# Down projection of an MLP as 2x2 blocks with seven products, its sums shared between VectorE and GpSimd

## The chip, the cores and the metric

The kernel runs on one core of a Trainium2 chip. The metric is the device time of one execution in microseconds; a kernel's time is the median of its runs. Engine names in the profile: PE is TensorE's matmuls, PEld its weight loads, DVE is VectorE, ACT is ScalarE, POOL is GpSimd, SP is SyncE, which issues most of the DMAs.

## The reference

One layer of a hybrid block on 512 tokens of width 2048: a gated-DeltaNet group and an RWKV-7 group, an output projection, cross attention to 256 memory tokens, and an MLP. What matters here is the end of it:

```python
D_MODEL = 2048; SEQ = 512; D_FF = 4 * D_MODEL
def reference(...):
    ...
    hn = _rmsnorm(h, norm_mlp[l])
    h = h + jnp.square(jax.nn.relu(hn @ mlp_w_up[l])) @ mlp_w_down[l]
    return _rmsnorm(h, norm_final)
```

All inputs and the output are float32. The kernel keeps that precision by splitting each operand of a product into a high part and a residue (lo = x - hi) and adding three matmuls: hi x hi, hi x lo, lo x hi.

## The kernel before

Everything is held transposed: features on the 128 partitions, the 512 tokens along the free dimension. The residual stream is 16 tiles `hres[n]` of 128x512.

**Splitting.** `split` writes the high part on ScalarE (L125, a cast) and the residue on VectorE (L126, a subtraction of two SBUF tiles). Weights come as raw tiles of 128x1024 (`wraw`, three buffers) and are split into `whi` and `wlo`, two buffers each, so the split of one block of weights can only start when TensorE has done with the block before the last. `mm` (L117) is the matmul, so all matmuls of the later stages have that line.

**Up** (strassen, 32 blocks `up0` to `up31`) multiplies 2x2 blocks with seven products instead of eight (Winograd's form). The blocks are halves of the tokens (`HA`, `HB`, 256 columns each) against pairs of feature rows. The sums of weights and of products are on VectorE (L1335). In the blocks 4 to 30 the products are "wide": high and low part of the activation lie side by side in one tile and one matmul takes 512 columns for hi x (hi, lo). In the others all matmuls have 256 columns, three for each weight block. Each result is squared and written to memory (`Ud`).

**Down** has eight parts of 1024 hidden rows, `e` = 0 to 7. The parts 0 to 6 are plain products: for each of the 16 output tiles `n`, the weights `w_dn[e, n]` are loaded and split, 24 matmuls of 512 columns go into one bank of PSUM (`dn{e}_{n}`), and VectorE adds the bank to `hres[n]` (L1722). Between these, `usplit` reads back the next part's hidden activations, multiplies them by `rstd` on VectorE (L1681) and splits them (`uh`, `ul`, 32 buffers of 128x512 under the name `act`, 24 more under `actb`). Part 7 goes token half by token half, so that the final norm and the output can begin early.

**Order of work.** Up and the parts 0 to 6 of down are put in order by a scheduler that takes the instructions as the code issues them and moves an engine's instruction ahead when its operands are there. Each engine then works its own queue strictly in order. Part 7 has its VectorE and ScalarE order as written. Tiles of one name share a fixed number of buffers, and a new tile waits until the readers of the old one are done.

GpSimd works in the first third only: prefix scans and masks of the two mixers.

Of the kernel before, what the change touches and what calls it, by code (L numbers as in the profile page):

```python
# [9 lines left out]
F32 = mybir.dt.float32  # L10
F32R = mybir.dt.float32r
AF = mybir.ActivationFunctionType
ALU = mybir.AluOpType
# [4 lines left out]
P = 128  # L18
T = 512
M = 256  # L20
KD = 16
# [52 lines left out]
def build(tc, I, out):  # L74
    nc = tc.nc
    V, S, GP, PE = nc.vector, nc.scalar, nc.gpsimd, nc.tensor
# [36 lines left out]
    def psb(nm, tag="mx", bufs=2):  # L113
        return tile_of(ps, [P, 512], F32, tag, nm, bufs)
# [29 lines left out]
    def wload(src):  # L144
        raw = wraw()
        nc.sync.dma_start(raw if len(src.shape) == 2 else raw.rearrange("p (a b) -> p a b", b=P), src)
        hi, lo = wsplit()
        split(raw, hi, lo)
        return hi, lo

    def gemm(pt, wsrc, nk, hi, lo):
        for h in range(nk // 8):
            wh, wl = wload(wsrc[:, h * 1024:(h + 1) * 1024] if nk > 8 else wsrc)
            for kk in range(8):
                k = h * 8 + kk
                sl = slice(kk * P, (kk + 1) * P)
                mm(pt, wh[:, sl], hi[k], start=(k == 0), stop=False)
                mm(pt, wh[:, sl], lo[k], start=False, stop=False)
                mm(pt, wl[:, sl], hi[k], start=False, stop=(k == nk - 1))
# [174 lines left out]
    def act_tile(nm, dt=F32R):  # L334
        return tile_of(pa, [P, 512], dt, "act", nm, 32)
# [5 lines left out]
    rstd = pc.tile([P, T], F32, name="rstd")  # L341
# [4 lines left out]
    cnt = [0]  # L346
# [87 lines left out]
    acc = tl("r")  # L434
# [807 lines left out]
    pm_cm.__exit__(None, None, None)  # L1242
    pq_cm.__exit__(None, None, None)
    ph = es.enter_context(tc.tile_pool(name="ph", bufs=1, reuse_waits="tile"))
    hres = [ph.tile([P, T], F32, tag=f"h{k}", name=f"h{k}", bufs=1) for k in range(16)]

    def btile(nm, dt=F32R):
        return ph.tile([P, 512], dt, tag="actb", name=nm, bufs=24)
# [11 lines left out]
    HA, HB = slice(0, M), slice(M, 2 * M)  # L1260
    comb = [[None] * 8 for _ in range(7)]

    B11, T1, T2, T3, T4, B22, B21 = range(7)
# [152 lines left out]
    banks, wts = {}, {}  # L1416
# [63 lines left out]
    for s in range(64):  # L1480
# [8 lines left out]
        if s > 1 and vsteps[s - 2][0] == "v" and vsteps[s - 2][2]:  # L1489
            n = vsteps[s - 2][1]  # L1490
# [92 lines left out]
    for g in range(2):  # L1583
        banks = (("mm", 2), ("mg", 2), ("mg", 2), ("mm", 2)), (("scr", 1), ("scg", 1), ("mm", 2), ("mm", 2))
        pts = [psb(f"sc{g}_{t}", *banks[g][t]) for t in range(4)]
        for n2 in range(8):
            cnt[0] += 1
            raw = pw.tile([P, 1024], F32, tag="wraw", name=f"kqr{cnt[0]}", bufs=NWR)
# [83 lines left out]
    def usplit(f):  # L1672
        if f >= 8:
            r = sl2()
        elif f % 2:
            r = ph.tile([P, T], F32, tag="acc", name=f"ur{f}", bufs=1)
        else:
            r = pu.tile([P, T], F32, tag="ur", name=f"ur{f}", bufs=1)
        nc.sync.dma_start(r, Ud[f // 2][:, f % 2, :])
        if f >= 8:  # L1680
            V.tensor_tensor(out=r, in0=r, in1=rstd, op=ALU.mult)  # L1681
        hi, lo = act_tile(f"uh{f}"), act_tile(f"ul{f}")
        if f < 56:
            split(r, hi, lo)
        else:
            for t, half in ((hi, HA), (lo, HB)):
                split(r[:, half], t[:, HA], t[:, HB])
        uhl[0].append(hi)
        uhl[1].append(lo)
# [3 lines left out]
    for p in range(32):  # L1693
# [9 lines left out]
        def used(i):  # L1703
# [5 lines left out]
            if p == 31 and i in (T1, T2, T3):  # L1709
                for f in (range(0, 3), range(3, 6), range(6, 8))[i - T1]:  # L1710
# [1 line left out]

        strassen(f"up{p}", (pu, 1024), [I["w_up"][p, i] for i in range(4)], list(range(8)), square, used, p == 0,
                 range(7) if 3 < p < 31 else ())
    for e in range(7):
        uh, ul = uhl[0][e * 8:], uhl[1][e * 8:]
        for n in range(KD):
            if n % 2 == 0:
                usplit(e * 8 + 8 + n // 2)
            pt = psb(f"dn{e}_{n}", "mm", 2)  # L1720
            gemm(pt, I["w_dn"][e, n], 8, uh, ul)
            V.tensor_tensor(out=hres[n], in0=hres[n], in1=pt, op=ALU.add)  # L1722

# [7 lines left out]
    def multiply(s):  # L1733

        n, half = where_[s]
        outs[s] = pt = psb(f"dn7_{s}", "mm", 2)
        wh, wl = wts[s]
        u = uhl[half is HB][56:]
        for k in range(8):
            sl = slice(k * P, k * P + P)  # L1740
            if s < 31:
                mm(pt, wh[:, sl], u[k], start=k == 0, stop=False)
            else:
                mm(pt[:, HA], wh[:, sl], u[k][:, HA], start=k == 0, stop=False)
                mm(pt[:, HA], wh[:, sl], u[k][:, HB], start=False, stop=False)
            mm(pt[:, HA], wl[:, sl], u[k][:, HA], start=False, stop=k == 7)
# [26 lines left out]
                               op0=ALU.mult, op1=ALU.mult)  # L1773
        (nc.sync if n % 2 or half is HA else nc.scalar).dma_start(out[n][:, half], h)

    wts[0] = wload(I["w_dn"][7, 0])
    for s in range(32):
        if s:
            collect(s - 1)
        if s < 31:  # L1780
            wts[s + 1] = wload(I["w_dn"][7, where_[s + 1][0]])
        if s:
            squared(s - 1)
            summed(s - 1)
        multiply(s)
        if s == 17:
            S.activation(rstd[:, HA], total(HA, sqs[15]), AF.Ln, bias=b_eps6, scale=1.0 / 2048)
        elif s == 18:
            S.activation(rstd[:, HA], rstd[:, HA], AF.Exp, scale=-0.5)
            ready += range(KD)  # L1790
        elif s == 22:
            S.activation(rcol[:, 0:1], rstd[:, 0:1], AF.Ln)
        for _ in range((s > 18) + (18 < s < 24)):
            if ready:
                scaled(ready.pop(0), HA)
# [10 lines left out]
def layout(inputs):  # L1806
    a = {k: np.asarray(v) for k, v in inputs.items()}
    f = np.float32
    D = 2048
    GW = 1024  # L1810
    d = {}
    d["xT"] = np.ascontiguousarray(a["x"][0].T.reshape(16, P, T).transpose(1, 0, 2))
    d["memT"] = np.ascontiguousarray(a["mem"][0].T.reshape(16, P, M).transpose(1, 0, 2))

    def tiles(w):
        kd, nd = w.shape[0] // P, w.shape[1] // P
        return np.ascontiguousarray(
            w.reshape(kd, P, nd, P).transpose(2, 1, 0, 3).reshape(nd, P, kd * P))

    w = a["w_in"][0]  # L1820
    r0 = 4 * GW + 16
    zero = lambda n: np.zeros((D, n), f)
    o0 = r0 + 3 * GW
    blocks = [w[:, o0:o0 + 128], w[:, o0 + 128:o0 + 256],
              w[:, o0 + 256:o0 + 288], w[:, 4 * GW:4 * GW + 8], zero(24),
              w[:, 4 * GW + 8:4 * GW + 16], zero(56)]
    for j in range(8):
        s = slice(j * P, (j + 1) * P)
        blocks += [w[:, r0:][:, s], w[:, r0 + GW:][:, s], w[:, r0 + 2 * GW:][:, s]]
        blocks += [w[:, i * GW:][:, s] for i in (1, 0, 2, 3)]  # L1830
    d["w_in"] = tiles(np.concatenate(blocks, 1))

    prm = np.zeros((P, NPRM), f)

    def put(name, arr, rows=slice(0, P)):
        o, n = PRM[name]
        prm[rows, o:o + n] = arr

    cols = lambda v: v.reshape(-1, P).T
    for n in ("norm_mix", "norm_xattn", "norm_mem", "norm_mlp"):  # L1840
        put(n, cols(a[n][0]))
    put("norm_final", cols(a["norm_final"]))
    mu = a["rwkv_mu"][0]
    mt = np.zeros((27, P), f)
    mt[0] = mu[3072:3200]
    mt[1] = mu[3200:3328]
    mt[2, :32] = mu[3328:3360]
    for j in range(8):
        for i in range(3):
            mt[3 + 3 * j + i] = mu[i * GW + j * P:i * GW + (j + 1) * P]  # L1850
    put("mu", mt.T)
    for n, k in (("w0", "rwkv_w0"), ("a0", "rwkv_a0"), ("kk", "rwkv_k_k"), ("ka", "rwkv_k_a"),
                 ("lnw", "rwkv_ln_w"), ("lnb", "rwkv_ln_b")):
        put(n, cols(a[k][0]))
    put("rk", cols(a["rwkv_r_k"][0].reshape(-1)))
    cw = a["gdn_conv_w"][0]
    put("conv", cw.reshape(4, 24, P).transpose(2, 1, 0).reshape(P, 96))
    put("gnw", a["gdn_norm_w"][0].reshape(P, 1))
    put("dtb", a["gdn_dt_bias"][0].reshape(8, 1), slice(32, 40))
    put("alog", a["gdn_A_log"][0].reshape(8, 1), slice(32, 40))  # L1860
    d["prm"] = prm
    d["cst"] = constants()
    d["w2a2"] = np.concatenate([a["rwkv_w2"][0], a["rwkv_a2"][0]], 0)
    g2 = a["rwkv_g2"][0]
    d["g2a"] = np.ascontiguousarray(g2[:128])
    d["g2b"] = np.ascontiguousarray(g2[128:])
    d["wk"] = tiles(a["xattn_wk"][0])
    d["wv"] = tiles(a["xattn_wv"][0])
    d["wqT"] = tiles(np.ascontiguousarray(a["xattn_wq"][0].T))
    wo = a["xattn_wo"][0]  # L1870
    d["wo"] = np.ascontiguousarray(
        wo.reshape(4, 4, P, 4, 512).transpose(3, 0, 2, 1, 4).reshape(4, 4, P, 2048))

    def blocks7(w):

        v = w.reshape(w.shape[0] // 256, 2, P, w.shape[1] // 256, 2, P)
        t = [v[:, k, :, :, m].transpose(2, 1, 0, 3) for m, k in ((0, 0), (1, 0), (1, 1), (0, 1))]
        return np.ascontiguousarray(np.stack(t, 1).reshape(w.shape[1] // 256, 4, P, -1))

    d["w_out"] = blocks7(a["w_out"][0])  # L1880
    d["w_up"] = blocks7(a["mlp_w_up"][0])
    wd = a["mlp_w_down"][0]
    d["w_dn"] = np.ascontiguousarray(
        wd.reshape(8, 8, P, 16, P).transpose(0, 3, 2, 1, 4).reshape(8, 16, P, 1024))
    return d


# [14 lines left out]
```

## Time and profile before

| | us |
|---|---|
| runs (3): median, lowest, highest | 2997.26, 2996.05, 2998.96 |
| profiled execution | 2995.97 |
| its span, first to last instruction | 2994.2 |
| mean granted TensorE clock | 0.999 |

| engine | busy us | share of the span |
|---|---|---|
| PE | 2963.1 | 99% |
| PEld | 2501.3 | 84% |
| DVE | 2125.9 | 71% |
| ACT | 1452.6 | 49% |
| POOL | 209.6 | 7% |

All times in lines of the profile count from the span's start. A line of a group reads: source line, engine, operation, out<-in by the program's names, shapes, count, then busy us and mean ns of one, then the idle time of the engine before these and who ended it. A line of the order in time reads: start, duration, engine, line, operation, out<-in. Matmuls are pipelined, so their pace is read from their starts. An instruction of VectorE is recorded with its tail, which overlaps the start of the next.

### The profile page before, as it was taken

How to read it: one execution, taken by the hardware profiler on the slowest of the kernel's cores; microseconds unless marked ns; L12 is line 12 of the kernel's file. 1: busy time of each engine (PE TensorE's matmuls, PEld its weight loads, DVE VectorE, ACT ScalarE, POOL GpSimd, SP SyncE). 2: the span in 40 equal slices, each digit the busy share in tenths (PEclk: the TensorE clock that was granted, in tenths of full speed). 3: DMA queues.
4: the chain of work that ended last, by engine and by line, in shares of the span. 5: the costliest groups of instructions: out<-in, count | busy, mean ns of one | idle time of the engine just before them, and what ended most of it. 6: DMA issues, size and time to landing. Idle time of an engine off the chain costs nothing.

```text
span 2994.2 us, 49167 instructions
## 1 busy us (share of the span) xinstructions
PE 2963.1 (99%) x19420; PEld 2501.3 (84%) x19420; DVE 2125.9 (71%) x3390; ACT 1452.6 (49%) x2133; POOL 209.6 (7%) x547
## 2 busy tenths in 40 slices
PE   9999999999999999999999999999999999999998
PEld 7887877877878888789978988888888888888887
DVE  7676676676778667679748999999997444444458
ACT  6455555555556565654446555555554222222234
POOL 0212311311312000000000000000000000000000
PEclk9999999999999999999999999999999999999999
DMA  5333333433435597763323444344444333333345
GB/s 183 105 89 81 104 88 83 103 87 82 130 89 164 176 280 244 257 227 126 104 79 99 148 135 141 128 134 140 132 137 159 127 127 103 115 126 127 116 127 183
DMA packets 226999, 402.91 MB, mean 135 GB/s; under 512 B 91912, under 2 KB 115724, under 8 KB 226768
## 3 DMA queue, kind: packets, MB, share of 16 engines
q1 hardware_dynamic: 211792, 373.54, 40.7%
q10 hardware_dynamic: 14976, 26.22, 2.3%
q8 instruction: 153, 2.51, 0.4%
q14 instruction: 78, 0.64, 0.1%
HBM read 352.10 MB, written 47.59 MB: 133 GB/s over the span
## 4 chain that ended last, share of the span: by engine, by line
PE 90%; DMA 2%; DVE 2%; ACT 1%; issue 1%; POOL 0%; ACTq 0%; SPq 0%; DVEq 0%; POOLq 0%
PE dn L117 23%; PE up L117 21%; PE py L244 18%; PE op L117 5%; PE kq L244 3%; PE vp L117 3%; PE at L117 3%; PE sc L117 3%; PE kp L244 3%; DMA wraw<-in_wo 1%; PE vo L117 1%; PE rs L244 1%; PE gs L244 1%; ACT whi L125 1%; PE pgB L244 0%
## 5 line engine op out<-in xcount | busy, mean ns | idle before, releaser
L125 ACT CAST whi<-wraw 128x1024 fp32r<-128x1024 f32 x384 | 404.0, 1052 | 758.6 <-PE dn L117 440.0
L126 DVE TENSOR_TENSOR wlo<-wraw,whi 128x1024 fp32r<-128x1024 f32 x384 | 469.3, 1222 | 75.3 <-ACT whi L125 72.5
L117 PE MATMUL up<-cb,whi 128*128 128x512 f32 (+1 forms) x2072 | 453.1, 363 | 0.8 <-ACT whi L125 0.8
L117 PE MATMUL dn<-ul,whi 128*128 128x512 f32 (+1 forms) x1032 | 394.0, 388 | 0.0
L117 PE MATMUL dn<-uh,whi 128*128 128x512 f32 x1024 | 393.8, 390 | 0.0
L117 PE MATMUL dn<-uh,wlo 128*128 128x512 f32 (+1 forms) x1024 | 384.5, 375 | 0.0
L117 PEld LDWEIGHTS up<-cb,whi 128*128 128x128 f32 x2072 | 342.2, 190 | 50.4 <-ACT whi L125 1.0
L244 PE MATMUL py<-xhi,whi 128*128 128x512 f32 x928 | 372.9, 402 | 6.8 <-ACT xhi L244 6.8
L244 PE MATMUL py<-xlo,whi 128*128 128x512 f32 x928 | 374.0, 403 | 0.3 <-DVE xlo L244 0.3
L244 PE MATMUL py<-xhi,wlo 128*128 128x512 f32 x928 | 373.1, 402 | 0.0
L1722 DVE TENSOR_TENSOR h<-h,dn 128x512 f32<-128x512 f32 x112 | 76.9, 686 | 298.4 <-PE dn L117 298.4
L244 DVE TENSOR_TENSOR wlo<-wraw,whi 128x1024 fp32r<-128x1024 f32 (+1 forms) x180 | 222.3, 1235 | 84.1 <-ACT whi L244 79.3
L244 ACT CAST whi<-wraw 128x1024 fp32r<-128x1024 f32 (+1 forms) x180 | 188.1, 1045 | 192.1 <-PE py L244 137.8
L117 PEld LDWEIGHTS up<-cb,wlo 128*128 128x128 f32 x1792 | 242.8, 191 | 16.1 <-DVE wlo L126 1.4
L117 PE MATMUL up<-cb,wlo 128*128 128x256 f32 x1792 | 251.2, 282 | 1.2 <-DVE wlo L126 1.2
L117 PEld LDWEIGHTS dn<-ul,whi 128*128 128x128 f32 x1032 | 193.2, 188 | 39.9
L117 PEld LDWEIGHTS dn<-uh,whi 128*128 128x128 f32 x1024 | 192.2, 188 | 40.9
L117 PEld LDWEIGHTS dn<-uh,wlo 128*128 128x128 f32 x1024 | 192.3, 188 | 35.1 <-DVE wlo L126 0.2
L244 PEld LDWEIGHTS py<-xhi,whi 128*128 128x128 f32 x928 | 175.1, 189 | 42.7 <-ACT xhi L244 7.2
L1335 DVE TENSOR_TENSOR sl<-sl,up 128x256 f32<-128x256 f32 x440 | 175.3, 417 | 45.7 <-PE up L117 43.2
L244 PEld LDWEIGHTS py<-xlo,whi 128*128 128x128 f32 x928 | 175.0, 189 | 35.7 <-DVE xlo L244 1.5
L244 PEld LDWEIGHTS py<-xhi,wlo 128*128 128x128 f32 x928 | 175.1, 189 | 34.4 <-issue 2.1
(848 smaller groups left out, 5195.8 us busy)
## 6 DMA issues: line engine op xcount, KB each, us to landing
wraw<-in_w_dn SPq DMA_DIRECT2D x144, 512.0 KB, 3.5
wraw<-in_w_up SPq DMA_DIRECT2D x128, 512.0 KB, 3.6
wraw<-in_w_in SPq DMA_DIRECT2D x116, 512.0 KB, 3.7
wraw<-in_wk SPq DMA_DIRECT2D x32, 512.0 KB, 3.6
wraw<-in_wqT SPq DMA_DIRECT2D x32, 512.0 KB, 5.2
wraw<-in_wv SPq DMA_DIRECT2D x32, 512.0 KB, 4.7
wraw<-in_wo SPq DMA_DIRECT2D x32, 512.0 KB, 5.7
wraw<-in_w_out SPq DMA_DIRECT2D x32, 512.0 KB, 3.6
```

Of the source, the lines that this page charges most:

```text
L117: PE.matmul(o, l, r, start=start, stop=stop)
L125: S.copy(hi, src)
L126: V.tensor_tensor(out=lo, in0=src, in1=hi.bitcast(F32), op=ALU.subtract)
L244: f(*a, **k)
L1335: V.tensor_tensor(out=o, in0=a, in1=b, op=op)
L1722: V.tensor_tensor(out=hres[n], in0=hres[n], in1=pt, op=ALU.add)
```

## The change

The parts 1 to 6 of down become 2x2 blocks with seven products.

- A *unit* is one part and one group `g` of four output tiles. Its four weight blocks (`w_dm`, 128x1024 each) are loaded raw; VectorE makes three sums of them (L1793, L1795, L1804), GpSimd one difference (L1799). Each of the seven products splits its weights and issues 24 matmuls of 256 columns into one bank of PSUM, two output tiles side by side.
- The results: `p1` and `p5` are copied out of PSUM by ScalarE, `u2` and `u3` are made by VectorE (L1782) from PSUM and a copy; GpSimd adds these copies to the residual, six additions of 512 columns a unit (L1778); VectorE adds `p2`, `p3` and `p4` from PSUM itself.
- The activations of the next part are made beside the unit (`downpair`): read back, multiplied by `rstd` on GpSimd (L1733), four differences on GpSimd (L1737), seven splits of 256 columns on ScalarE and VectorE.
- The residual tiles lie in pairs, `hp[i]` of 128x2x512, so that one addition reaches two output tiles in one token half.
- Part 0 stays plain, with the first `downpair` groups beside it; part 7 is the same with other indices. The multiplications by `rstd` that `usplit` did on VectorE go to GpSimd.

```diff
-    hres = [ph.tile([P, T], F32, tag=f"h{k}", name=f"h{k}", bufs=1) for k in range(16)]
+    hp = [ph.tile([P, 2, T], F32, tag=f"h{i}", name=f"h{i}", bufs=1) for i in range(8)]
+    hres = [hp[k // 4 * 2 + k % 2][:, k // 2 % 2] for k in range(16)]
...
         if f >= 8:
-            V.tensor_tensor(out=r, in0=r, in1=rstd, op=ALU.mult)
+            GP.tensor_tensor(out=r, in0=r, in1=rstd, op=ALU.mult)
...
-    for e in range(7):
-        uh, ul = uhl[0][e * 8:], uhl[1][e * 8:]
-        for n in range(KD):
-            if n % 2 == 0:
-                usplit(e * 8 + 8 + n // 2)
-            pt = psb(f"dn{e}_{n}", "mm", 2)
-            gemm(pt, I["w_dn"][e, n], 8, uh, ul)
-            V.tensor_tensor(out=hres[n], in0=hres[n], in1=pt, op=ALU.add)
+    def downpair(e, k):
+        eo = [pu.tile([P, T], F32, tag="ur", name=f"de{e}_{k}", bufs=1),
+              ph.tile([P, T], F32, tag="acc", name=f"do{e}_{k}", bufs=1)]
+        for j, r in enumerate(eo):
+            nc.sync.dma_start(r, Ud[e * 4 + k][:, j, :])
+        for r in eo:
+            GP.tensor_tensor(out=r, in0=r, in1=rstd, op=ALU.mult)
+        a, b = eo
+        def gsub(o, x, y):
+            GP.tensor_tensor(out=o, in0=x, in1=y, op=ALU.subtract)
+        for i, src, sums in ((B11, a[:, HA], None), (B21, b[:, HA], None), (B22, b[:, HB], None),
+                             (T1, a[:, HA], (a[:, HB], a[:, HA])), (T2, a[:, HA], (b[:, HB], a[:, HA])),
+                             (T3, a[:, HB], (b[:, HB], a[:, HB])), (T4, a[:, HA], (b[:, HA], a[:, HA]))):
+            if sums:
+                gsub(src, *sums)
+            t = dcomb[e][i][k]
+            split(src, t[:, HA], t[:, HB])
+            yield
+    def downunit(e, g, aside):
...
+        def product(i, a, tag):
+            hi, lo = wsplit()
+            split(a, hi, lo)
+            pt = psb(f"d{e}_{g}_{i}", tag, 2)
+            for q in range(2):
+                o = pt[:, q * M:q * M + M]
+                for k in range(4):
+                    sl = slice(q * 512 + k * P, q * 512 + k * P + P)
+                    c = dcomb[e][i][k]
+                    mm(o, hi[:, sl], c[:, HA], start=q + k == 0, stop=False)
+                    mm(o, hi[:, sl], c[:, HB], start=False, stop=False)
+                    mm(o, lo[:, sl], c[:, HA], start=False, stop=q == 1 and k == 3)
+            next(aside, None)
+            return pt
+        def add(m, half, src, eng, op=ALU.add):
+            h = hp[2 * g + m][:, :, half]
+            eng.tensor_tensor(out=h, in0=h, in1=two(src), op=op)
...
+        p1 = product(B11, a11, "mm")
+        s1, s2 = ws(), ws()
+        V.tensor_tensor(out=s1, in0=a21, in1=a22, op=ALU.add)
+        p2 = product(B21, a12, "mg")
+        V.tensor_tensor(out=s2, in0=s1, in1=a11, op=ALU.subtract)
+        u1 = copied(p1)
+        add(0, HA, u1, GP)
+        p6 = product(T2, s2, "mx")
+        GP.tensor_tensor(out=a21, in0=a11, in1=a21, op=ALU.subtract)
+        add(0, HA, p2, V)
+        p5 = product(T1, s1, "mm")
+        u2 = summed(u1, p6)
+        add(0, HB, u2, GP)
+        V.tensor_tensor(out=a12, in0=a12, in1=s2, op=ALU.subtract)
+        p7 = product(T3, a21, "mg")
+        c5 = copied(p5)
+        add(0, HB, c5, GP)
+        add(1, HB, c5, GP)
+        p3 = product(B22, a12, "mx")
+        u3 = summed(u2, p7)
+        add(1, HA, u3, GP)
+        add(1, HB, u3, GP)
+        p4 = product(T4, a22, "mm")
+        add(0, HB, p3, V)
+        add(1, HA, p4, V)
...
+    for e in range(1, 7):
+        if e < 6:
+            downplaces(e + 1)
+        for g in range(4):
+            beside = aside(e, g)
+            downunit(e, g, beside)
+            for _ in beside:
+                pass
```

`summed` is one VectorE addition and `copied` one ScalarE copy into a tile of `sl` (three buffers). In part 6 `aside` runs `usplit` for part 7 instead of `downpair`: two multiplications on GpSimd and four residues of 256 columns a unit.

More of the change, by code (lines that the diff above doesn't have):

```diff
@@ L1680, in usplit @@
         if f >= 8:
-            V.tensor_tensor(out=r, in0=r, in1=rstd, op=ALU.mult)
-        hi, lo = act_tile(f"uh{f}"), act_tile(f"ul{f}")
+            GP.tensor_tensor(out=r, in0=r, in1=rstd, op=ALU.mult)
+        hi, lo = (act_tile(f"uh{f}"), act_tile(f"ul{f}")) if f < 8 else (place_(), place_())
         if f < 56:
@@ L1714, in build, with place_ @@
                  range(7) if 3 < p < 31 else ())
-    for e in range(7):
-        uh, ul = uhl[0][e * 8:], uhl[1][e * 8:]
-        for n in range(KD):
-            if n % 2 == 0:
-                usplit(e * 8 + 8 + n // 2)
-            pt = psb(f"dn{e}_{n}", "mm", 2)
-            gemm(pt, I["w_dn"][e, n], 8, uh, ul)
-            V.tensor_tensor(out=hres[n], in0=hres[n], in1=pt, op=ALU.add)
+    DORD = (B11, B21, T2, T1, T3, B22, T4)
+    dcomb, taken = {}, [16]
+    def place_():
+        taken[0] += 1
+        return (act_tile if (taken[0] - 1) % 56 < 32 else btile)(f"dc{taken[0]}")
@@ new lines, in downunit, with raw, ws, summed @@
+    def downunit(e, g, aside):
+        def raw(i):
+            cnt[0] += 1
+            r = wraw() if i in (0, 3) else pu.tile([P, 1024], F32, tag="wraw2", name=f"dr{cnt[0]}", bufs=3)
+            nc.sync.dma_start(r, I["w_dm"][e - 1, g, i])
+            return r
+        def ws():
+            cnt[0] += 1
+            return pu.tile([P, 1024], F32, tag="ws", name=f"dws{cnt[0]}", bufs=2)
+        def product(i, a, tag):
[12 more added lines that the diff above has]
+            return pt
+        two = lambda a: a.rearrange("p (q t) -> p q t", t=M)
+        def add(m, half, src, eng, op=ALU.add):
+            h = hp[2 * g + m][:, :, half]
+            eng.tensor_tensor(out=h, in0=h, in1=two(src), op=op)
+        def summed(a, b):
+            o = sl2()
+            V.tensor_tensor(out=o, in0=a, in1=b, op=ALU.add)
+            return o
+        def copied(a):
+            o = sl2()
+            S.copy(o, a)
+            return o
+        a11, a12, a21, a22 = raw(0), raw(3), raw(1), raw(2)
+        p1 = product(B11, a11, "mm")
[23 more added lines that the diff above has]
+        add(1, HA, p4, V)
@@ new lines, in aside, with downplaces @@
+    def aside(e, g):
+        if e < 6:
+            yield from downpair(e + 1, g)
+        else:
+            for f in (56 + 2 * g, 57 + 2 * g):
+                usplit(f)
+                yield
+                yield
+    def downplaces(e):
+        dcomb[e] = {i: [place_() for _ in range(4)] for i in DORD}
+    downplaces(1)
+    for n in range(KD):
+        if n % 4 == 0:
+            beside = aside(0, n // 4)
+        pt = psb(f"dn0_{n}", "mm", 2)
+        gemm(pt, I["w_dn"][0, n], 8, *uhl)
+        V.tensor_tensor(out=hres[n], in0=hres[n], in1=pt, op=ALU.add)
+        for _ in range(2):
+            next(beside, None)
@@ L1727, in build @@
+    for e in range(1, 7):
+        if e < 6:
+            downplaces(e + 1)
[4 more added lines that the diff above has]
+                pass
     order = tc.manual_schedule(engines={nc.vector.engine, nc.scalar.engine})
@@ L1737, in multiply @@
         wh, wl = wts[s]
-        u = uhl[half is HB][56:]
+        u = uhl[half is HB][8:]
         for k in range(8):
@@ L1774, in scaled @@
         (nc.sync if n % 2 or half is HA else nc.scalar).dma_start(out[n][:, half], h)
-    wts[0] = wload(I["w_dn"][7, 0])
+    wts[0] = wload(I["w_dn"][1, 0])
     for s in range(32):
@@ L1780, in build @@
         if s < 31:
-            wts[s + 1] = wload(I["w_dn"][7, where_[s + 1][0]])
+            wts[s + 1] = wload(I["w_dn"][1, where_[s + 1][0]])
         if s:
@@ L1883, in layout @@
     d["w_dn"] = np.ascontiguousarray(
-        wd.reshape(8, 8, P, 16, P).transpose(0, 3, 2, 1, 4).reshape(8, 16, P, 1024))
+        wd.reshape(8, 8, P, 16, P).transpose(0, 3, 2, 1, 4).reshape(8, 16, P, 1024)[[0, 7]])
+    v = wd.reshape(8, 4, 2, P, 4, 2, 2, P)[1:7]
+    t = [v[:, :, k, :, :, :, m].transpose(0, 3, 2, 4, 1, 5) for m, k in ((0, 0), (1, 0), (1, 1), (0, 1))]
+    d["w_dm"] = np.ascontiguousarray(np.stack(t, 2).reshape(6, 4, 4, P, 1024))
     return d
```

## The prediction

> **What bounds the kernel now.** I read the page first: the engines' busy shares, and the chain of waits that ended last.
>
> ```profile
> PE 2963.1 (99%) x19420; PEld 2501.3 (84%) x19420; DVE 2125.9 (71%) x3390; ACT 1452.6 (49%) x2133; POOL 209.6 (7%) x547
> PE dn L117 23%; PE up L117 21%; PE py L244 18%; PE op L117 5%; PE kq L244 3%; PE vp L117 3%; PE at L117 3%; PE sc L117 3%; PE kp L244 3%; DMA wraw<-in_wo 1%; PE vo L117 1%; PE rs L244 1%; PE gs L244 1%; ACT whi L125 1%; PE pgB L244 0%
> ```
>
> TensorE is busy for 99% of the span, and the multiplications of down (dn) are 23% of the chain, the largest piece. Next I looked at that stage alone: busy time by stretches (columns: length, then busy us and count of PE, weight load, DVE, ACT, POOL; clock, DMA share, GB/s), the instructions that touch dn, and what TensorE waits for from 2279 us to the end.
>
> ```profile
> core 0: us, PE busy (x) PEld busy (x) DVE busy (x) ACT busy (x) POOL busy (x), PEclk, DMA share, GB/s
> 2300.00:2400.00 100.00, 100.00 (x443) 82.78 (x442) 46.73 (x58) 24.69 (x27) 0.00 (x0) 1.00 0.38 123
> 1660.00:1720.00 60.00, 58.14 (x481) 57.82 (x482) 55.43 (x72) 31.93 (x48) 0.00 (x0) 1.00 0.44 141
> L1722 DVE TENSOR_TENSOR h<-h,dn x112: 678/687/689, 2284.8 to 2888.7; 128x512 f32<-128x512 f32 x112
> PE pss L117 <- ACT sl L1757: 0.6, 1, 0.6
> ```
>
> In down TensorE never stops (100.00 of 100.00), VectorE is under half busy, GpSimd does nothing, and the only wait of TensorE in the whole stretch is 0.6 us. So here time is the number of matmuls times their pace, and anything that takes matmuls away gains until another engine fills up. The pace comes from L1722, one addition for each output tile: 112 of them, first to last 2888.7 - 2284.8 = 603.9 us, so 603.9 / 111 = 5.44 us a tile, 16 tiles = 87.05 us a part, and **the six parts that change take 522.3 us today**.
>
> **What TensorE does after the change.** A unit (one part, four output tiles) is seven products of 24 matmuls with 256 columns; six parts have 24 units. The up stage already runs such products in its last block, seen in time order on TensorE:
>
> ```profile
> 2263.76 1.12 PE L117 MATMUL up<-cb,wlo 128*128 128x256 f32 x8
> 2264.72 2.08 PE L117 MATMUL up<-cb,whi 128*128 128x256 f32 x16
> 2266.64 1.12 PE L117 MATMUL up<-cb,wlo 128*128 128x256 f32 x8
> ```
>
> From one group of 8 to the next, 24 matmuls pass in 2266.64 - 2263.76 = 2.88 us, 0.12 us each, so their weight loads do not hold them up. A unit is 7 x 2.88 = 20.16 us and 24 units are 483.8 us: 38.5 us less than 522.3. If TensorE stays the bound, that is the whole effect.
>
> **What the other engines must do in those 20.16 us.** The durations come from back-to-back VectorE instructions in time order, and from the groups by line and shape:
>
> ```profile
> 2099.94 1.08 DVE L1335 TENSOR_TENSOR sl<-sl,up 128x256 f32<-128x256 f32 x3 [0.43 <-PE up L117]
> 2107.39 1.22 DVE L1335 TENSOR_TENSOR ws<-wraw,wraw 128x1024 f32<-128x1024 f32 x1
> 2108.53 1.22 DVE L126 TENSOR_TENSOR wlo<-wraw,whi 128x1024 fp32r<-128x1024 f32 x1
> 2109.66 1.22 DVE L1335 TENSOR_TENSOR wraw<-wraw,wraw 128x1024 f32<-128x1024 f32 x1
> 2294.65 1.89 DVE L1681 TENSOR_TENSOR sl<-sl,rstd 128x512 f32<-128x512 f32 x3
> L125 ACT CAST whi<-wraw 128x1024 fp32r<-128x1024 f32 x384 | 404.0, 1052 | 758.6 <-PE dn L117 440.0 <-PE up L117 172.2 <-PE op L117 37.1
> L1267 ACT CAST cb<-sl 128x256 fp32r<-128x256 f32 x56 | 20.3, 401 | 19.5 <-DVE sl L1271 19.5
> L1467 ACT COPY sl<-vo 128x512 f32<-128x512 f32 x32 | 18.6, 582 | 10.1 <-DMA vod<-sl 5.1 <-ACT sl L1467 5.1
> L1268 DVE TENSOR_TENSOR cb<-sl,cb 128x256 fp32r<-128x256 f32 x56 | 21.7, 419 | 4.5 <-ACT cb L1267 4.5
> L244 POOL TENSOR_TENSOR gEs<-gE,cst 128x512 f32<-128x512 f32 x8 | 10.3, 1289 | 0.3 <-ACT gE L244 0.3
> L244 POOL TENSOR_TENSOR sr<-sr,sr 64x63 f32<-64x63 f32 x16 | 4.8, 301 | 1.3
> ```
>
> VectorE's 128x1024 starts follow each other by 1.135 us (2107.39, 2108.53, 2109.66); for 256 columns the step is (1.08 - 0.42) / 2 = 0.33, for 512 it is (1.89 - 0.69) / 2 = 0.60. A unit of the parts 1 to 5 has seven weight residues (L126) and three weight sums of 1024 columns, 10 x 1.135 = 11.35; seven residues of the next part's activation blocks, 7 x 0.33 = 2.31; five additions out of PSUM, 5 x 0.60 = 3.0. Sum 16.7 us, under 20.16. ScalarE: 7 x 1.05 + 7 x 0.40 + 2 x 0.58 = 11.3 us, under half of what would matter. GpSimd: six additions into the residual and two multiplications by rstd of 512 columns, 8 x 1.29 = 10.32; one weight difference of 1024 and four activation differences of 256, which the trace does not show: between 63 and 512 columns the two rows grow by 988 / 449 = 2.2 ns a column, which puts them at 2.42 and 0.73, so 2.42 + 2.92. Sum 15.7 us. Counted engine by engine, all fit, and the 38.5 us would be gained.
>
> **The cost that this count misses.** VectorE and GpSimd have so far seldom met. Where they do, in the first third of the kernel, the order in time shows:
>
> ```profile
> 118.74 0.69 DVE L244 TENSOR_TENSOR y<-py,rstd 128x512 f32<-128x512 f32 x1 [0.49 <-PE py L244]
> 119.59 2.18 DVE L244 TENSOR_TENSOR wlo<-wraw,whi 128x1024 fp32r<-128x1024 f32 x1 [0.16 <-ACT whi L244]
> 118.79 0.65 POOL L244 COPY sr<-sr 64x256 f32<-64x256 f32 x1
> 119.41 1.28 POOL L244 TENSOR_TENSOR gEs<-gE,cst 128x512 f32<-128x512 f32 x1
> ...
> 898.09 2.25 DVE L244 TENSOR_TENSOR wlo<-wraw,whi 128x1024 fp32r<-128x1024 f32 x1 [3.53 <-ACT whi L244]
> 897.97 1.29 POOL L244 TENSOR_TENSOR gEs<-gE,cst 128x512 f32<-128x512 f32 x1
> ...
> 448.73 1.23 DVE L244 TENSOR_TENSOR wlo<-wraw,whi 128x1024 fp32r<-128x1024 f32 x1 [1.81 <-ACT whi L244]
> 448.50 0.21 POOL L244 TENSOR_TENSOR sr<-sr 64x15 f32<-64x15 f32 x1
> 448.78 1.25 POOL L244 TENSOR_TENSOR sr<-sr,sr 64x15 f32<-64x15 f32 x1
> ```
>
> The residue that takes 1.22 us took 2.25 when GpSimd's 128x512 had begun 0.12 us before it: it stood until 898.09 + 1.03 = 899.12, which is 0.14 us before GpSimd's end. The 2.18 us case gives the same: 119.59 + 0.96 = 120.55 against an end of 120.69. The other way round, a GpSimd instruction of 15 columns, 0.21 us long, took 1.25 when a residue had begun 0.05 us before it. So whichever comes second waits for nearly the whole of the first. The addition that takes one operand from PSUM (y<-py,rstd) kept its 0.69 us beside GpSimd's 64x256 copy. The Trainium skill (SBUF — State Buffer, "Who interferes with whom") has a rule that speaks against this change: a VectorE instruction with two SBUF inputs and a GpSimd instruction that reads SBUF exclude each other for the whole instruction, while one SBUF input is harmless. The trace agrees, except for the 0.14 us; with GpSimd's whole durations the sum below would be 710 instead of 665 us, an end at 3185.
>
> All of a unit's GpSimd work reads two SBUF tiles, and so does all of VectorE's except its five PSUM additions. **They need one resource in turn.** VectorE holds it for 11.35 + 2.31 = 13.66 us. GpSimd holds it for its durations less 0.14 each: 15.7 - 13 x 0.14 = 13.8. Together 27.5 us a unit where TensorE needs 20.16. The PSUM additions (3.0) lie beside GpSimd's turns and are not counted. In part 6 the activation differences fall away, and GpSimd has 8 x 1.29 + 2.42 - 9 x 0.14 = 11.5, VectorE 11.35 + 4 x 0.33 = 12.7: 24.2 us a unit. Twenty units at 27.5 and four at 24.2 are 646 us. Turns are not gapless: each weight residue waits for its cast, and where VectorE was 92% busy with the same kind of product (1660 to 1720, above) TensorE lost 1.86 of 60 us, 3%. With 3% the six parts take **665 us, 143 more than 522**.
>
> The bounds of this sum. Upwards, GpSimd's whole duration excludes VectorE and the PSUM additions find no cover: 13.66 + 15.7 + 3.0 = 32.4 a unit, 12.7 + 12.7 + 3.0 = 28.4 in part 6, 762 us in all, +239. Downwards, GpSimd's fixed start also lies beside VectorE: 2.2 ns x 63 = 0.14 of the 0.30 us row is columns, so 0.16 is start, 13.8 - 2.1 = 11.7 and 25.4 a unit, 22.7 in part 6, 599 us, +77. I take the middle, since the two rows with 0.14 are the only direct measure.
>
> **The rest costs nothing.** Part 0 keeps its matmuls; beside it GpSimd gets four groups of 2 x 1.29 + 4 x 0.73 = 5.5 us and VectorE 28 residues of 0.33, against 87 us in which VectorE now works 47%. Part 7 is the same with other indices. The 56 multiplications by rstd leave VectorE (L1681) where it had room. Weight transfers stay 16 of 512 KB a part at a DMA share of 0.38. The activations of six parts are read back in the same transfers as before. What is queued behind a wait: ScalarE's cast of an activation block waits for GpSimd's difference, and the weight cast behind it waits too; GpSimd's difference overwrites its input and waits for VectorE's residue of the block before. These rounds make the losses of the rival below.
>
> **The sum.** The profiled execution took 2995.97 us (span 2994.2), 1.3 under the median of 2997.26. 2995.97 + 143 + 1.3 = **3140 us**. About 0.2%, 6 us, is what a measurement of this kernel can tell from no change.
>
> **Rivals.**
> 1. *TensorE stays the bound (faster).* Place: GpSimd's 128x512 additions. If VectorE gets in between their columns, the change keeps its 38.5 us: 2957.5, or 2972 with 3% lost. It decides when GpSimd's hold falls from 13.8 to 20.16 - 13.66 = 6.5 us a unit. For it: of long GpSimd instructions against long residues the trace has two meetings only. Against: both show a full wait. Chance 0.10.
> 2. *Turns overlap by half.* Half of the 7.3 us over 20.16 is hidden: 23.8 and 22.2 a unit, 565 us, +43: 3040. Nothing in the trace shows half a wait, but few instructions were tried. Chance 0.08, with 0.02 more around no change.
> 3. *The in-order queues, not the shared resource, set the pace.* There are two buffers for a split weight, so the split for product i+2 starts when product i ends. Cast 1.05, residue 1.22, one PSUM addition 0.69, one activation residue 0.42 and three of GpSimd's turns of 1.15 ahead of it are 6.83 us; two products then take 2.88 + 6.83, one 4.86, a unit 34 us, 24 units 816: 3291. It decides above 4.97 us of split time. For it: the waits of ScalarE on GpSimd named above. Against: three turns between two residues is more than the 13 to 17 ratio of their counts. Chance 0.12.
> 4. *Narrow matmuls save nothing.* Ruled out by 0.12 us for each in the up rows.
>
> **How the numbers follow.** The forecast, 3074 to 3236 by its own bounds, has 0.68. The range, 3055 to 3265, takes it in with the top of rival 2 and the bottom of rival 3, and leaves out some 0.2. Faster by over 0.2% is rival 1, 0.10; within 0.2%, 0.02; slower, 0.68 + 0.08 + 0.12 = 0.88.
>
> **What would show it.** In the profile after: TensorE's busy share over down near 75%, waiting for wlo (L126) and whi; weight residues in down at a mean near 1.8 us instead of 1.22 while five PSUM additions stay at 0.69; GpSimd's 512-column additions well over 1.29; one unit every 27 to 28 us. It is wrong if the residues stay at 1.22 us beside GpSimd's additions, or if units pass in 20 us; and wrong in size, by rival 3, if both engines stand idle together for a third of a unit.

## The result

The changed kernel takes 3168.09 us (median of 5; 3165.46 to 3169.72) against 2996.05 before: ratio 1.0572, 95% interval 1.0558 to 1.0585, **172 us slower**. The forecast was 3140, inside 3055 to 3265. The profiled execution took 3165.76 us, its span is 3164.0, 169.8 more than before.

The page of the profile after, busy shares and chain:

```profile
PE 2996.8 (95%) x21148; PEld 2599.6 (82%) x21148; DVE 2464.2 (78%) x3622; ACT 1580.7 (50%) x2373; POOL 745.0 (24%) x867
PE 71%; DVE 8%; POOL 7%; DMA 4%; issue 3%; ACT 3%; ACTq 0%; POOLq 0%; DVEq 0%; SPq 0%
```

The same chain before, by engine:

```profile
PE 90%; DMA 2%; DVE 2%; ACT 1%; issue 1%; POOL 0%; ACTq 0%; SPq 0%; DVEq 0%; POOLq 0%
```

TensorE's share of the chain falls from 90% to 71%; VectorE and GpSimd, 2% and 0% before, now hold 15% of it. Two lines place the loss: the stretch of the six parts and the pace in it, by stretches and by the instructions that touch the products; and the last addition of part 0.

```profile
core 0: us, PE busy (x) PEld busy (x) DVE busy (x) ACT busy (x) POOL busy (x), PEclk, DMA share, GB/s
2376.00:3058.00 682.00, 550.23 (x4024) 528.56 (x4024) 568.03 (x507) 249.02 (x365) 498.84 (x289) 0.92 0.27 89
L117 PE MATMUL d<-dc,wlo x1344: 277/283/583, 2375.1 to 3057.9; 128*128 128x256 f32 x192
L1836 DVE TENSOR_TENSOR h<-h,dn x16: 674/680/689, 2284.8 to 2375.8; 128x512 f32<-128x512 f32 x16
```

The six parts take 683 us where they took 522: +161. Part 0's first addition is where it was, at 2284.8; its last comes at 2375.8 instead of 2284.8 + 15 x 5.44 = 2366.4: +9. Together 170, the whole difference. The groups of the stretch 2366 to 3060, by shape:

```profile
L1778 POOL TENSOR_TENSOR h<-h,sl 128x512 f32<-128x512 f32 x144 | 270.1, 1889 | 63.9 <-ACT sl L1787 36.9 <-DVE sl L1782 27.0
L126 DVE TENSOR_TENSOR wlo<-wraw,whi 128x1024 fp32r<-128x1024 f32 x75 | 122.6, 1635 | 26.8 <-ACT whi L125 26.8
L126 DVE TENSOR_TENSOR wlo<-dr,whi 128x1024 fp32r<-128x1024 f32 x48 | 81.5, 1699 | 8.9 <-ACT whi L125 8.9
L1799 POOL TENSOR_TENSOR dr<-wraw,dr 128x1024 f32<-128x1024 f32 x23 | 69.5, 3020 | 3.5 <-DVE dws L1793 3.5
L1795 DVE TENSOR_TENSOR dws<-dws,wraw 128x1024 f32<-128x1024 f32 x23 | 61.7, 2681 | 0.0
L1778 DVE TENSOR_TENSOR h<-h,d 128x512 f32<-128x512 f32 x72 | 48.8, 678 | 13.7 <-POOL h L1778 13.2 <-PE d L117 0.5
```

Everything with two operands in SBUF has become longer: residues 1.64 and 1.70 us instead of 1.22, the weight sum L1795 2.68, GpSimd's additions 1.89 instead of 1.29. VectorE's additions out of PSUM are at 0.678, unchanged. The order in time of one stretch shows it happen:

```profile
2719.44 0.68 DVE L1778 TENSOR_TENSOR h<-h,d 128x512 f32<-128x512 f32 x1
2720.03 1.71 DVE L1795 TENSOR_TENSOR dws<-dws,wraw 128x1024 f32<-128x1024 f32 x1
2721.67 3.39 DVE L126 TENSOR_TENSOR wlo<-wraw,whi 128x1024 fp32r<-128x1024 f32 x1
2724.99 0.67 DVE L1778 TENSOR_TENSOR h<-h,d 128x512 f32<-128x512 f32 x1
...
2716.26 4.41 POOL L1778 TENSOR_TENSOR h<-h,sl 128x512 f32<-128x512 f32 x2 [0.96 <-DVE sl L1782]
2720.62 3.36 POOL L1799 TENSOR_TENSOR dr<-wraw,dr 128x1024 f32<-128x1024 f32 x1
2723.94 2.27 POOL L1733 TENSOR_TENSOR do<-do,rstd 128x512 f32<-128x512 f32 x1
```

The residue at 2721.67 finds GpSimd's 1024-column difference under way and takes 3.39 us; that difference had itself waited for the sum at 2720.03. The two additions out of PSUM pass beside GpSimd at full pace.

How much of the stretch the turns fill can be worked out from the same trace. A GpSimd instruction or a VectorE instruction with two operands in SBUF is under way in 639 of the 682 us (overlaps counted once; the prediction counted 646). In the other 43 us neither is, and in 21 of these VectorE and GpSimd both do nothing at all. What TensorE waits for in the stretch:

```profile
PE d L117 <- DVE wlo L126: 114.2, 79, 3.1
PE d L117 <- ACT whi L125: 16.9, 10, 2.5
```

### The profile page after: what moved, and what is told of

Read it like the earlier page. It is cut to its first block, busy times and chain, and to the rows that moved or that the text cites. A ratio compares the mean times of both kernels' runs of the same rounds, so it can differ in the third digit from the quotient of the medians.

```text
span 3164.0 us, 53596 instructions
## 1 busy us (share of the span) xinstructions
PE 2996.8 (95%) x21148; PEld 2599.6 (82%) x21148; DVE 2464.2 (78%) x3622; ACT 1580.7 (50%) x2373; POOL 745.0 (24%) x867
## 4 chain that ended last, share of the span: by engine, by line
PE 71%; DVE 8%; POOL 7%; DMA 4%; issue 3%; ACT 3%; ACTq 0%; POOLq 0%; DVEq 0%; SPq 0%
PE up L117 19%; PE py L244 17%; PE op L117 5%; PE dn L117 4%; PE d L117 4%; DVE wlo L126 4%; POOL h L1778 3%; PE kq L244 3%; PE vp L117 3%; PE at L117 3%; PE sc L117 3%; PE kp L244 2%; POOL de L1737 2%; DVE dc L126 1%; ACT whi L125 1%
## 5 line engine op out<-in xcount | busy, mean ns | idle before, releaser
L125 ACT CAST whi<-wraw 128x1024 fp32r<-128x1024 f32 x360 | 378.0, 1050 | 460.3 <-PE up L117 175.2
L117 PE MATMUL d<-dc,whi 128*128 128x256 f32 x2688 | 525.8, 297 | 16.9 <-ACT whi L125 16.9
L117 PE MATMUL d<-dc,wlo 128*128 128x256 f32 x1344 | 410.1, 305 | 114.9 <-DVE wlo L126 114.2
L117 PEld LDWEIGHTS d<-dc,whi 128*128 128x128 f32 x2688 | 451.2, 206 | 19.3 <-ACT whi L125 19.2
L117 PEld LDWEIGHTS d<-dc,wlo 128*128 128x128 f32 x1344 | 276.5, 206 | 134.2 <-DVE wlo L126 134.0
L1733 POOL TENSOR_TENSOR de<-de,rstd 128x512 f32<-128x512 f32 x24 | 37.8, 1574 | 1350.2 <-DMA wraw<-in_w_dn 1331.9
L1778 POOL TENSOR_TENSOR h<-h,sl 128x512 f32<-128x512 f32 x144 | 270.1, 1889 | 63.9 <-ACT sl L1787 36.9
L125 ACT CAST whi<-ws 128x1024 fp32r<-128x1024 f32 x120 | 126.1, 1051 | 102.8 <-PE up L117 61.5
```

The source lines that it names most:

```text
L117: PE.matmul(o, l, r, start=start, stop=stop)
L125: S.copy(hi, src)
L1733: GP.tensor_tensor(out=r, in0=r, in1=rstd, op=ALU.mult)
L1778: eng.tensor_tensor(out=h, in0=h, in1=two(src), op=op)
```

## The experiments

The theory: VectorE instructions with two operands in SBUF and GpSimd instructions that read SBUF take turns, and the sum of the turns (27.5 us a unit) sets the pace. The rivals: the in-order queues, with ScalarE's casts waiting for GpSimd (rival 3 of the prediction), and the halved clock (granted 0.92 in the stretch above). The time of one unit is the span from the first to the last matmul of the six parts divided by 24; after the change that span is 683 us. Kernels without an interval ran once, beside the kernel before on the same chip.

**VectorE off the shared resource.**

```diff
-            split(a, hi, lo)
+            S.copy(hi, a)
+            for c in (slice(0, 512), slice(512, 1024)):
+                V.tensor_tensor(out=lo[:, c], in0=still, in1=hi[:, c].bitcast(F32), op=ALU.subtract)
```

> The residue of a unit's weights takes its first operand from a bank of PSUM that holds a constant, in two instructions of 512 columns, so the products of the six parts are not the reference's; GpSimd's work, the queues and all waits on the casts stay. If VectorE's two-SBUF instructions and GpSimd's exclude each other, VectorE needs its turn only for 3 x 1.135 + 7 x 0.33 = 5.7 us a unit, with GpSimd's 13.8 that is 19.5, under TensorE's 20.16: units of 20.2 to 21.5 us instead of 28.5, 2970 to 3000 us in all, residues back at 0.69 each. If the in-order queues set the pace (casts waiting for GpSimd's differences), units stay above 27 us and the time above 3130. If the halved clock is the cause and not a consequence, it stays halved for about a sixth of the stage and the time above 3120.

3025.78 us (before: 2996.89). The six parts take 545 us, 22.7 a unit: 138 of the 161 us are gone, with GpSimd's work untouched. The residues do not wait any more, the remaining two-SBUF sums do (groups of 2380 to 2850; line numbers shifted by the edit):

```profile
L1763 DVE TENSOR_TENSOR wlo<-still,whi 128x512 fp32r<-128x512 f32 x292 | 186.6, 678 | 6.7 <-ACT whi L1761 6.6
L1797 DVE TENSOR_TENSOR dws<-dws,wraw 128x1024 f32<-128x1024 f32 x21 | 51.6, 2459 | 0.0
2373.00:2918.00 545.00, 499.44 (x4031) 487.23 (x4030) 488.23 (x675) 249.59 (x366) 408.00 (x290) 1.00 0.34 112
```

The clock is back at 1.00 by itself. The unit is 1.2 us and the time 26 us over the top of what was expected: the sum of turns, 19.5, was not the bound any more, and VectorE is at 488 of 545 us, with its other two-SBUF work still waiting (2.46 us for 1.22). The waits of the queues are still there: ScalarE waits 146 us for GpSimd's work on the next part's activations, and the stage is 138 us faster all the same.

```profile
ACT dc L125 <- POOL de L1737: 82.8, 66, 3.9
ACT dc L125 <- POOL do L1733: 36.2, 15, 3.6
ACT dc L125 <- POOL de L1733: 27.2, 17, 3.1
```

**GpSimd off it.** Each GpSimd instruction of the units and pairs becomes two memsets, later three:

```diff
-            GP.tensor_tensor(out=r, in0=r, in1=rstd, op=ALU.mult)
+            GP.memset(r, 0.0)
+            GP.memset(r, 0.0)
```

> Every GpSimd instruction of the units and of the activation pairs is replaced by two memsets of its output, which read nothing, so the products and the residual of the six parts are not the reference's; order, buffers and waits stay. Shared turns: if only GpSimd's reads exclude VectorE, units fall to 20.2 to 22 us and the time to 2970 to 3010, and VectorE's residues to 1.22. Queues: GpSimd still stands between ScalarE and VectorE at the same places with about 1.1 us instead of 1.3 alone, so the units stay above 26 us, above 3110. If GpSimd's writes exclude VectorE as well, it lands between, near 3090.

> As with the memsets before, but three for each GpSimd instruction, so that GpSimd works 6 x 1.58 + 2.87 + 2 x 1.58 + 4 x 0.93 = 19.2 us a unit by the memsets' measured 0.526, 0.957 and 0.311 us: longer than the 15.7 that its additions need alone; still nothing is read, and the products and the residual of the six parts are not the reference's. Shared turns on reads: VectorE's residues stay at 1.22 us, 2970 to 3000 us. If the gain with two memsets came from shorter GpSimd work, the waits for GpSimd come back: above 3080.

2969.56 us, 0.4 under its range, and 2985.12 us, inside its range (before: 2996.89 and 2994.14). Six parts: 496 and 507 us, 20.7 and 21.1 a unit against TensorE's 20.16. By stretches, two memsets and then three, and a residue of the second:

```profile
2366.00:2861.00 495.00, 489.25 (x4025) 484.41 (x4024) 411.03 (x509) 249.57 (x367) 234.09 (x470) 1.00 0.37 123
2371.00:2877.00 506.00, 491.81 (x4027) 486.24 (x4027) 414.43 (x509) 247.24 (x367) 351.83 (x750) 1.00 0.37 120
L126 DVE TENSOR_TENSOR wlo<-dr,whi 128x1024 fp32r<-128x1024 f32 x45 | 55.0, 1222 | 6.0 <-ACT whi L125 6.0
```

GpSimd is busy for 352 of 506 us, close to what its additions need alone in this stretch (24 x 10.16 + 20 x 5.5 + 8 x 1.29 = 364), and as long as it reads nothing it costs VectorE next to nothing: all weight residues of this kernel have means of 1.22 to 1.26 us. By themselves these two kernels do not part the reading from the queues. A memset that stands for an addition waits for no copy, and the scheduler moved about a third of these memsets (about a fifth with three) ahead of the six parts; ScalarE's waits for GpSimd's work on the next part's activations fell to 45 us (58 with three), from 201 in the change. The first experiment has those waits, 146 us of them. The two together settle the main cause: it is GpSimd's reading beside VectorE's, not its place in the queues.

**The rounds cut.** GpSimd's multiplications and differences for the next part go to a tile that nobody reads:

```diff
-                gsub(src, *sums)
+                gsub(idle, *sums)
```

> GpSimd does the same multiplications and differences for the next part's activations but writes them to a tile that nobody reads (the multiplications as two of 256 columns, 0.3 us more a unit), and the splits take the activations as read back; the activations of the six parts are not the reference's. GpSimd's load stays, the rounds GpSimd to ScalarE to VectorE to GpSimd and ScalarE's waits for GpSimd are gone. Shared turns: 13.66 + 14.1 us a unit as before, so 3150 to 3180. Queues: the casts behind those waits come in time, units of 24 to 25 us, 3080 or less. In between, the share of each can be read off.

3198.99 us, 31 slower than the change, and over the range of both theories. ScalarE's waits for the pair work had been 201 us (83.9 + 65.0 + 52.4):

```profile
ACT dc L125 <- POOL de L1737: 83.9, 45, 4.4
ACT dc L125 <- POOL do L1733: 65.0, 14, 9.0
ACT dc L125 <- POOL de L1733: 52.4, 15, 7.7
```

Now 85 us are left, and for the reading back (the pair has one buffer, which GpSimd must be done with first):

```profile
ACT dc L125 <- DMA do<-ud: 72.3, 15, 11.7
ACT dc L125 <- DMA de<-ud: 12.9, 13, 2.5
```

More than half of the waits gone and no gain: the rounds do not set the pace of the change. The turns fill 641 us, as in the change (639); the 31 us are gaps between them, and this trace does not show whether the new waits for the reading back make them.

**GpSimd's instructions cut to 256 columns.**

```diff
+                for q in range(2):
+                    GP.tensor_tensor(out=h[:, q], in0=h[:, q], in1=src[:, q * M:q * M + M], op=op)
```

> The whole change with GpSimd's instructions cut to 256 columns: additions and multiplications in two, the weight difference in four. The work is the same, GpSimd's turns add up to 24 x 0.59 = 14.2 us a unit instead of 13.8. Sum of turns: 3165 to 3195. Long turns: each wait of a residue is halved, 3100 to 3150.

3195.47 us, 0.5 over the top of what the sum of turns said. Shorter waits for the same work gain nothing. The turns fill 667 us instead of 639, 28 more where the count said 10, and the time is 27 us longer. The sum counts, not the length of one turn.

**The clock.**

```diff
+            for k in range(6):
+                mm(idle, dcomb[e][i][k % 4][:, 0:P], dcomb[e][i][k % 4][:, HA])
```

> Six more matmuls of 256 columns stand ahead of each product of the six parts, into a spare bank that nobody reads: TensorE's work is 7 x 30 x 0.12 = 25.2 us a unit, its waits get shorter and the clock should stay at 1. If the halved clock costs time by itself, the time falls to 3110 to 3150. If the shared turns of VectorE and GpSimd set the pace, units stay at 28 to 29 us, 3155 to 3190.

3236.05 us, 68 slower and over both ranges, six parts in 748 us:

```profile
2380.00:3128.00 748.00, 650.79 (x5037) 634.26 (x5036) 565.96 (x508) 249.88 (x366) 488.44 (x289) 0.96 0.26 82
```

The clock rose from 0.92 to 0.96 and nothing was gained; the matmuls added are 24 x 7 x 6 x 0.12 = 121 us of work, and the six parts became 65 us longer. As a test it is not clean: the filler brought back only half of the lost clock and stood in the way of the products. What the halved clock costs of the 161 us stays open. TensorE lost at most 0.08 of 682 us by it, 55; and since the turns fill 639 us of the stretch, everything that is not a turn, the clock and the queues together, has at most the other 43.

That the clock follows from the waits can be read from the traces. The records show it granted at 1 or 0.5, in steps of 3.41 us. In the change, the step behind a full-clock step in which TensorE stood still for 1.90 us or more is at half clock, all 24 times, and no step behind one with 1.81 us or less is. In the first experiment no step has more than 1.50 us of standing still, and the clock is 1.00.

**Less on GpSimd.** Two other divisions of the work: all of GpSimd's work on VectorE, and the residual additions on VectorE out of PSUM.

```diff
-        add(0, HA, u1, GP)
+        add(0, HA, u1, V)
```

```diff
-        u2 = summed(u1, p6)
-        add(0, HB, u2, GP)
+        plus(p6, u1)
+        add(0, HB, p6, V)
+        u2 = copied(p6)
```

> All of GpSimd's work in down goes to VectorE, nothing else is changed. VectorE then works 16.7 + 6 x 0.60 + 1.135 + 2 x 0.60 + 4 x 0.33 = 24.0 us a unit, 21.6 in part 6: 566 us for the six parts, 600 with a few per cent lost. Shared turns: 3040 to 3080, faster than the change although one engine does the work of two. If the sharing is sound and the loss lies in the block products or their buffers, VectorE as the only engine makes it worse than the change: above 3168.

> The six additions to the residual leave GpSimd for VectorE and take their operand from PSUM, where u2 and u3 are made in place; ScalarE copies u1 and u2. VectorE then works 13.66 + 11 x 0.60 = 20.3 us a unit, of which the 6.6 out of PSUM need no turn; GpSimd keeps the weight difference and the activation pairs, 6.9 us of turns. Shared turns: 20.6 us a unit at best, 24.9 if VectorE waits for GpSimd in proportion to its two-SBUF share (6.9 x 13.66 / 20.3 = 4.6): six parts in 493 to 588 us, 2970 to 3070 in all. Queues alone: ScalarE's waits for GpSimd's differences stay, so above 3100.

3061.41 us (ratio 1.0225, 1.0209 to 1.0240) and 3075.66 (1.0263, 1.0246 to 1.0280), before 2994.14. **One engine doing the work of two is 107 us faster than the two sharing it.** By stretches, the first and the second:

```profile
2363.00:2957.00 594.00, 525.69 (x4033) 504.36 (x4032) 565.34 (x797) 253.56 (x365) 0.00 (x0) 0.97 0.32 103
2376.00:2971.00 595.00, 525.26 (x4028) 507.02 (x4027) 542.43 (x652) 251.63 (x366) 203.48 (x146) 0.96 0.32 102
```

Without GpSimd, the six parts take 594 us against 566 counted for VectorE, which is busy for 95% of the stretch: it is the bound, and part 0 ends without loss (the six parts begin at 2363 instead of 2375). The second misses its range by a little (595 us against 588 for the six parts, 3075.66 against 3070): 24.8 us a unit, as if GpSimd's 6.9 us of turns had fallen on VectorE's two-SBUF work in proportion. That is a fit and no test of it. Neither beats the kernel before. A unit must get under 522.3 / 24 = 21.8 us; VectorE alone needs 24.0, and what GpSimd takes from it comes back as waits.

**Half of the turns.** The six additions left out, then variants of that kernel: the weight difference in four pieces, the rounds cut, a third pair of weight buffers.

```diff
-        add(0, HA, u1, GP)
...
-        add(1, HB, u3, GP)
```

> GpSimd's six additions to the residual are left out, so the output lacks p1, u2, p5 and u3 of the six parts; the activation pairs, the weight difference and all casts and waits on them stay. Shared turns: GpSimd holds 6.9 us a unit instead of 13.8, with VectorE's 13.66 that is 20.6; VectorE's own 16.7 and waits of up to 6.9 x 13.66 / 16.7 = 5.6 make 22.3: 492 to 535 us for the six parts, 2975 to 3020 in all. Queues: the rounds between GpSimd, ScalarE and VectorE are all there, so units above 26 us and the time above 3100.

> As without the six additions (3070), with GpSimd's weight difference cut into four instructions of 256 columns; the output again lacks p1, u2, p5 and u3 of the six parts. Without the additions the turns add up to only 20.6 us a unit, yet a unit took 24.5, so something beside their sum costs 4 us. Theory of the long turn: a residue that comes behind a 1024-column difference waits 2.3 us, more than the product before it gives it, and TensorE stops; with pieces of 0.6 us units fall to 22 to 23 us, 3010 to 3040. Theory of the rounds between GpSimd, ScalarE and VectorE: nothing changes, 3060 to 3085.

> Without the six additions, and with the multiplications and differences of the activation pairs written to a tile that nobody reads, so that ScalarE and VectorE never wait for GpSimd's pair work; the activations of the six parts are not the reference's and the output lacks p1, u2, p5 and u3. Rounds: the 4 us a unit that the sum of turns leaves open vanish, units of 20.5 to 22 us, 2980 to 3020. Long turns: they stay, 3055 to 3090.

> Without the six additions, and with a third pair of buffers for split weights (in two instructions of 512 columns); to make room, all six parts multiply with part 1's activations and the next part's are split into tiles that nobody reads, so the output is not the reference's, while every instruction stays. Theory of the ring: with two buffers a split may start only when the product before the last is done, and cast and residue (1.05 + 1.22) leave 0.6 us of the product's 2.88 for any wait; with three they leave 3.5 us, so waits for GpSimd's turns are hidden: 20.5 to 22 us a unit, 2970 to 3015 us. If the open 4 us a unit come from the order of the queues (VectorE's other work ahead of the residues, late activations), units stay at 24 to 25 us, 3055 to 3085.

3070.52, 3059.24, 3085.30 and 3053.74 us; six parts in 588, 576, 599 and 573 us. The first misses both ranges: with turns of 20.6 us a unit takes 24.5. In its trace the turns fill 487 of 589 us (in the change 639 of 682). So where the turns no longer fill the time, their sum is not the pace. None of three single causes is it: short turns give 11 us, a third pair of buffers 17, cutting the rounds makes it 15 slower. The trace of the last shows what two of the waits look like, in the order in time on ScalarE, GpSimd and VectorE:

```profile
2604.10 0.71 ACT L125 CAST dc<-do 128x256 fp32r<-128x256 f32 x2 [3.46 <-POOL do L1733]
2604.72 1.04 ACT L125 CAST whi<-wraw 128x1024 fp32r<-128x1024 f32 x1
...
2604.03 3.39 POOL L1805 TENSOR_TENSOR dr<-wraw,dr 128x1024 f32<-128x1024 f32 x1
...
2602.85 2.30 DVE L126 TENSOR_TENSOR wlo<-dr,whi 128x1024 fp32r<-128x1024 f32 x1
2605.07 3.42 DVE L1802 TENSOR_TENSOR dws<-dws,wraw 128x1024 f32<-128x1024 f32 x1
```

A weight cast stands behind an activation cast that waits 3.46 us for GpSimd; and GpSimd's weight difference starts when VectorE's first sum is done, so the second sum mostly finds it under way (a median of 3.42 us over its 24 instances, for 1.22). Queue waits and turns mix here, and which share each has is open.

## Why the prediction was right, point by point

**TensorE's pace: right.** Units of 20.7 us where nothing reads against VectorE; 483.8 was the floor and 496 the best measured.

**The shared resource: right, and the step that carried the forecast.** It was read from three meetings in the trace of before. The marks named in advance came: residues at 1.64 to 1.70 us (1.8 forecast), additions out of PSUM at 0.678, GpSimd's additions at 1.89. Two marks came only roughly: a unit takes 28.5 us instead of 27 to 28, and TensorE's recorded busy share is 81% instead of near 75%, since matmuls at half clock are recorded as longer (up to 583 ns, where the median is 283). Taking GpSimd's reads away brings back TensorE's pace, and taking the residues' reads away brings back 138 of the 161 us. The rule of the Trainium skill (SBUF — State Buffer, "Who interferes with whom"), that only a GpSimd instruction that reads excludes a VectorE instruction with two SBUF inputs, and that one that only writes does not, agrees with the 1.22 us of the residues beside memsets.

**The sum: 665 us forecast, 683 measured.** Turns of 646 us hold (639 in the trace); the loss on top, taken as 3% from the up stage, was 37 us, 5.7%. That term is the mis-sized one: 19 us forecast, 37 measured. The up stage had no GpSimd beside it and no halved clock. The 18 us may lie in the clock, which the prediction left out: TensorE's waits reached 3.1 us and the granted clock fell to 0.92, while with waits of at most 1.5 us in the first experiment it stayed at 1.00. The Trainium skill (TensorE: Matmul & The Clock Gate, "The HAM clock gate") puts the halving after an idle window of about 3.4 us; here less was enough, 1.90 us of standing still within a step of 3.41. That these 18 us are the clock's is argued, not shown.

```profile
PE d L117 <- DVE wlo L1763: 38.9, 41, 1.5
```

**"Part 0 costs nothing": wrong, 9 us.** The cover named, VectorE at 47%, was there, and it did not help. ScalarE's weight cast stood behind activation casts that waited for GpSimd, in the stretch 2279 to 2376:

```profile
ACT dc L125 <- POOL de L1737: 15.5, 14, 2.6
ACT dc L125 <- POOL de L1733: 15.0, 5, 4.4
ACT dc L125 <- POOL do L1733: 8.6, 4, 2.6
```

The queue waits that the prediction kept for rival 3 act here, where no engine is full; with all work on VectorE part 0 loses nothing. GpSimd's reading is not needed for this loss: with three memsets, which read nothing but take longer than the instructions they replace (and some of the additions' lie in part 0 too), part 0's last addition starts 91.8 us after its first, as late as in the change (91.0); with two it is 80.2.

**The rivals.** TensorE staying the bound, and half-overlapped turns, are out. The queues alone are out as the cause of the change's time: the sign named for them was both engines idle together for a third of a unit, and they are for 21 of 682 us. But the kernels with half of the turns show that they take over as soon as the turns leave room: the turn sum is a lower bound there, not the pace.

## What to carry to other kernels

Before work is shared between VectorE and GpSimd, count not each engine's busy time but the time that both need SBUF's shared reads: all GpSimd instructions that read, and all VectorE instructions with two SBUF operands. That sum is a floor. If it is over the time that is to be met, sharing cannot meet it; if it is also over what the first engine would need alone (here 27.5 against 24.0 us a unit), the second engine makes it worse than leaving all on the first. A sum under the target promises nothing: with 20.6 us of turns a unit still took 24.5. A few meetings of the two engines in the trace of before were enough to see that they take turns.

## What was not expected of the hardware

A memset on GpSimd, 0.53 us for 128x512 (0.52 in the kernel before), runs beside VectorE's two-SBUF work at next to no cost to either side (residues of 1.22 to 1.26 us). And waits of 2 to 3 us, 1.90 us of standing still within one step of 3.41, are enough to halve TensorE's clock for the next step (0.92 granted over the stretch), although TensorE was busy for 550 of 682 us.
